# Split weight blocks of the projections: made once and kept in DRAM instead of made three times

## The chip, the cores and the metric

The kernel runs on one core of a Trainium2 chip. The metric is the device time of one execution in microseconds (us). The core has five engines with an instruction stream each: TensorE (PE, and PEld for its weight loads), VectorE (DVE), ScalarE (ACT), GpSimd (POOL) and SyncE (SP), which in this kernel issues nearly all DMA transfers. Each stream is worked off in order, and a semaphore wait of one instruction holds all that stand behind it.

## The reference

One layer of a decoder works on 2048 prompt tokens and on 8 sample sequences of 8 tokens, which share the weights. What is computed, in short:

```python
h    = rmsnorm(x, norm_mix_w)
proj = h @ w_in                                    # 1024 x 4096
rq, rk, rv, rg, hq, hf, hi, hg = split(proj, 8)    # 4 heads x 128 columns each
o_r  = retention(rotary(rq), rotary(rk), rv)       # decay 1 - 2^(-5-head), chunkwise
o_h  = hgrn2(silu(hq), 1 - f, hi, log(f))          # f = lb + (1 - lb) * sigmoid(hf)
o    = concat(head_rmsnorm(o_r) * silu(rg), head_rmsnorm(o_h) * silu(hg))
x    = x + o @ w_out                               # 1024 x 1024
x    = x + square(relu(rmsnorm(x, norm_ffn_w) @ w_up)) @ w_down
y    = rmsnorm(x, final_norm_w)
```

All of it is in float32. Results are y for both groups of tokens and the final states of both recurrences.

## The kernel before, in words

**Precision.** TensorE takes operands in a shorter format (fp32r). Each operand is therefore split into two parts: `hi`, the value rounded to fp32r, and `lo`, the rest. A product is three matmuls: hi x hi, hi x lo and lo x hi (`proj`, line 314).

**Groups.** The 2112 tokens are worked in three groups, each through the whole layer: group 0 (64 sample tokens and 512 prompt tokens), group 1 (768 prompt tokens) and group 2 (768). A group's activations stay on the chip. In each group come first the mix (for each of four heads p: `project` with four blocks of columns, `values` at line 672, and before the next head the two gate blocks, `gates`), then the output projection (`residual` at line 1110 with six weight blocks, and `out_proj_first` or `out_proj` with two), then the feed-forward part (`ffn_first` or `ffn`). `finish_first` and `finish`, the final norm of the group before, are spread over the first part of the next group's mix (DVE lines 1232 and 1605, stores of y at lines 1235 and 1607).

**The weight stream.** The weights lie in DRAM as blocks of 128 x 1024 float32, 512 KB each, in the order in which they are used; blocks 0 to 31 are the input projection's and 32 to 39 the output projection's (W_UP0 is 40). Every group uses these 40. `plan_stream` (line 273) lists all uses: 104 entries for group 0, then 149 for each of the others, in all 402. The feed-forward entries of groups 1 and 2 differ from those of group 0: they are for a product scheme with sums of blocks, which `plan_sums` forms during group 0 on VectorE (line 1256), stores in DRAM (line 1261) and which come back as entries of kind "s".

**What one entry costs.** `weight(i)` (line 242) is called when block i is about to be used, and it readies the blocks up to i + 2. For each: a DMA loads the block into a tile `raw` (line 251); ScalarE casts it to `hi` (line 256); VectorE or GpSimd subtracts, `lo = raw - hi` (line 271, `second_part`). GpSimd takes the subtraction where the entry says so, or, for the entries of these 40 blocks, where the stream number j is over 3 and not divisible by 4; VectorE takes the rest. `hi` and `lo` have three buffers each, so the cast of block i waits until TensorE has read block i - 3 for the last time. `raw` tiles have two buffers in group 0, and two and four more (tag `sum`) afterwards, where loads run further ahead.

**What uses two blocks at once.** `values` takes two blocks and holds both until its last matmul (line 687). All other uses take the blocks one after the other.

**Order.** Work beside the matmuls is put on an agenda counted in ticks (`at`, `later`, `tick`), a tick being a few matmuls. The framework then lays out each engine's instruction order with a time model of its own, from the order of the calls and from what is ready, with tiles taking their buffers in the order of the calls; `keep_in_program_order` pins single instructions behind what was called before on the same engine. All loads and stores that the prediction speaks of stand in the queue of SyncE.

**Lines that the prediction follows.** L610, L611 and L668: the halves of a projected key swapped on ScalarE, and times sine on GpSimd; L667 and L669: the rest of the rotation on VectorE. L823, L330, L331, L469 and L470: the product of query and key of the same token (GpSimd), its split (ScalarE, VectorE) and its column sums (TensorE). L777: the scan of the log gates on VectorE. L1292: the output projection's sums taken out of PSUM. L1588: sums of squares of the final norm on GpSimd.

Of the kernel before, what the change touches and what calls it, by code (L numbers as in the profile page):

```python
# [9 lines left out]
F32 = mybir.dt.float32  # L10
F32R = mybir.dt.float32r
# [4 lines left out]
P = 128  # L16
# [22 lines left out]
WT = 1024  # L39
N_IN, N_OUT, N_UP, N_DN = 32, 8, 32, 32  # L40
W_OUT0 = N_IN
W_UP0 = W_OUT0 + N_OUT
# [4 lines left out]
W_UQ0 = W_DN0 + N_DN  # L47
W_DQ0 = W_UQ0 + N_UP
NW = W_DQ0 + N_DN

# [91 lines left out]
def lay_out_weights(w_in, w_out, w_up, w_down):  # L144
    w = np.empty((NW, P, WT), np.float32)
    wi = w_in.reshape(KB, P, 8, H, DK)
# [51 lines left out]
class Kernel:  # L198
# [43 lines left out]
    def weight(self, i):  # L242
        n = len(self.stream)
        while self.w_next < min(i + 1 + self.ahead, n):
            j = self.w_next
            while self.w_load <= j or j >= self.n_first and self.w_load <= j + 2 and self.w_load < n:
                k, later = self.w_load, self.w_load >= self.n_first
                raw = self.raws[k] = self.wp.tile([P, WT], F32, tag="sum" if later and k % 3 else "raw", name="raw",
                                                  bufs=4 if later and k % 3 else 2)
                e = self.stream[k]  # L250
                self.fetch(raw, self.sums[e[1]] if e[0] == "s" else self.I["w"][e[1]])
                self.w_load += 1
            raw = self.raws.pop(j)
            hi = self.wp.tile([P, WT], F32R, tag="hi", name="hi")
            lo = self.wp.tile([P, WT], F32R, tag="lo", name="lo")
            self.nc.scalar.copy(hi, raw)  # L256
            self.wts[j] = (hi, lo)
            self.second[j] = raw
            pool = self.stream[j][2] if len(self.stream[j]) > 2 else j % 4 and 3 < j
            if pool or j < 4:  # L260
                self.second_part(j, self.nc.gpsimd if pool else self.nc.vector)
            else:
                self.later(4, self.second_part, j, self.nc.vector)
            self.w_next += 1
        self.second_part(i, self.nc.vector)
        return self.wts[i]
# [6 lines left out]
    def plan_stream(self):  # L273

        self.stream = [("w", j) for j in range(W_UP0)]
        up = [[("w", W_UP0 + 4 * t + i) for i in range(4)] for t in range(NQ)]
        dn = [[("w", W_DN0 + 4 * t + i) for i in range(4)] for t in range(NQ)]
        self.stream += up[0]
        for t in range(NQ):
            self.stream += (up[t + 1] if t < NQ - 1 else []) + dn[t]  # L280
        self.n_first = len(self.stream)

        def entry(name, key, i0, pool):
            return ("s", key + (name,), pool) if name[0] == "S" else ("w", i0 + A_PLACE[name], pool)

        for g in range(1, len(GROUPS)):
            self.stream += [("w", j) for j in range(W_UP0)]
            self.stream += [("w", W_UQ0 + i, i % 2) for i in range(4)]
            for t in range(1, NQ):
                self.stream += [entry(name, ("u", t), W_UQ0 + 4 * t, name in ("A12", "S1", "S4")) for name, _ in PRODUCTS]  # L290
            for o in range(NO):
                for k, (name, *_) in enumerate(LAST_OCTET if o == NO - 1 else OCTET):
                    end = g == len(GROUPS) - 1 and o == NO - 1 and k > 4
                    self.stream += [entry(name, ("d", o, v), W_DQ0 + 4 * (2 * o + v), not end and (2 * k + v) % 5 in (1, 3))
                                    for v in range(2)]

    def next_weight(self):
        i = self.w_use
        self.w_use += 1
        r = self.weight(i)  # L300
        self.wts.pop(i - 4, None)
        return r

# [45 lines left out]
    def build(self):  # L349
        nc, tc, I = self.nc, self.tc, self.I  # L350
        with ExitStack() as ctx:
# [10 lines left out]
            self.raws, self.sums, self.side = {}, {}, deque()  # L362
            self.ordered = True
            self.ahead = 2
            self.wts, self.second = {}, {}
            self.blocks = deque()
            self.plan_stream()

# [1365 lines left out]
```

## Time and profile before

| | |
|---|---|
| median of 3 runs | 2627.51 us |
| lowest and highest | 2626.79 and 2630.17 us |
| the profiled execution | 2629.84 us |
| its span, first to last instruction | 2628.0 us |
| mean granted TensorE clock | 0.995 |
| TensorE busy | 2570.6 us |
| VectorE, ScalarE, GpSimd busy | 1683.9, 1234.5, 1089.9 us |
| moved by DMA | 365.81 MB, mean 139 GB/s |

In this execution the groups lie as follows, by the first and last instructions of their lines: group 0's mix until about 300 us, its output projection until 368, its feed-forward part until 793; group 1's mix until about 1150, its output projection until 1222, its feed-forward part until 1697; group 2 from there.

A row of groups reads: line, engine, operation, output <- inputs, shapes, count; busy us in all, mean ns of one; idle us before them and what ended it. A row of the timeline reads: start, length, engine (a q behind it: its sequencer, such as SPq when a DMA is issued), line, operation, tiles, shapes, how many in a row, and in brackets the idle time before and what ended it. A row of the stretches gives the busy time of TensorE, its weight loads, VectorE, ScalarE and GpSimd (instructions in brackets), then the clock, the mean busy share of the 16 DMA engines and their GB/s. A matmul's time there is that from issue to end; neighbours overlap.

### The profile page before, as it was taken

How to read it: one execution, taken by the hardware profiler on the slowest of the kernel's cores; microseconds unless marked ns; L12 is line 12 of the kernel's file. 1: busy time of each engine (PE TensorE's matmuls, PEld its weight loads, DVE VectorE, ACT ScalarE, POOL GpSimd, SP SyncE). 2: the span in 40 equal slices, each digit the busy share in tenths (PEclk: the TensorE clock that was granted, in tenths of full speed). 3: DMA queues.
4: the chain of work that ended last, by engine and by line, in shares of the span. 5: the costliest groups of instructions: out<-in, count | busy, mean ns of one | idle time of the engine just before them, and what ended most of it. 6: DMA issues, size and time to landing. Idle time of an engine off the chain costs nothing. (4 is left out here: it accounts for less than half of the span.)

```text
span 2628.0 us, 41634 instructions
## 1 busy us (share of the span) xinstructions
PE 2570.6 (98%) x16999; PEld 2536.8 (97%) x16999; DVE 1683.9 (64%) x2077; ACT 1234.5 (47%) x1653; POOL 1089.9 (41%) x605
## 2 busy tenths in 40 slices
PE   8999999999999999999999999999999999999997
PEld 8999999999999999999999999989999999999997
DVE  6666776545565466565554988675665665549886
ACT  6555442222244555554543545455555445345443
POOL 6555557444436355431222332463554302223322
PEclk9999999999999999999999999999999999999999
DMA  5233366666752111122556755421111225566552
GB/s 181 81 97 90 121 217 241 232 252 221 266 183 85 57 49 49 53 66 69 166 174 203 261 169 199 145 97 49 46 44 59 70 69 178 179 207 209 175 178 81
DMA packets 125951, 365.81 MB, mean 139 GB/s; under 512 B 12480, under 2 KB 33984, under 8 KB 125760
## 3 DMA queue, kind: packets, MB, share of 16 engines
q1 hardware_dynamic: 125616, 363.13, 41.7%
q8 instruction: 134, 2.20, 0.3%
q14 instruction: 57, 0.47, 0.1%
q10 hardware_dynamic: 144, 0.02, 0.0%
HBM read 293.10 MB, written 69.99 MB: 138 GB/s over the span
## 5 line engine op out<-in xcount | busy, mean ns | idle before, releaser
L271 POOL TENSOR_TENSOR lo<-raw,hi 128x1024 fp32r<-128x1024 f32 x227 | 591.3, 2605 | 1257.6 <-ACT hi L256 1140.6
L323 PE MATMUL pj<-slab,hi 128*128 128x288 f32 (+1 forms) x5120 | 1016.8, 316 | 18.9 <-ACT hi L256 6.3
L323 PEld LDWEIGHTS pj<-slab,hi 128*128 128x128 f32 x5120 | 811.8, 189 | 25.2 <-ACT hi L256 9.3
L256 ACT CAST hi<-raw 128x1024 fp32r<-128x1024 f32 x402 | 422.3, 1052 | 847.1 <-PE pj L323 373.3
L323 PE MATMUL pj<-slab,lo 128*128 128x288 f32 (+1 forms) x2560 | 600.1, 315 | 1.8 <-POOL lo L271 1.7
L1105 PE MATMUL pd<-slab,hi 128*128 128x384 f32 x1792 | 457.2, 335 | 6.7 <-DVE slab L1551 3.1
L323 PEld LDWEIGHTS pj<-slab,lo 128*128 128x128 f32 x2560 | 430.0, 189 | 2.9 <-POOL lo L271 2.0
L1105 PE MATMUL pu<-slab,hi 128*128 128x384 f32 x1600 | 396.2, 334 | 0.0
L1105 PEld LDWEIGHTS pd<-slab,hi 128*128 128x128 f32 x1792 | 324.3, 188 | 8.4 <-DVE slab L1551 3.7
L271 DVE TENSOR_TENSOR lo<-raw,hi 128x1024 fp32r<-128x1024 f32 x175 | 231.6, 1323 | 156.0 <-ACT hi L256 152.7
L1105 PE MATMUL pd<-slab,lo 128*128 128x384 f32 x896 | 300.2, 335 | 0.9 <-POOL lo L271 0.9
L1105 PEld LDWEIGHTS pu<-slab,hi 128*128 128x128 f32 x1600 | 288.2, 188 | 0.0
L1105 PE MATMUL pu<-slab,lo 128*128 128x384 f32 x800 | 256.9, 334 | 0.0
L687 PE MATMUL pjv<-hi,slab 128*128 128x256 f32 x1088 | 211.6, 288 | 3.9 <-DVE slab L667 3.9
L1307 DVE TENSOR_TENSOR slab<-slab 128x768 fp32r<-128x768 f32 x144 | 162.3, 1143 | 41.4 <-ACT slab L1303 29.1
L687 PEld LDWEIGHTS pjv<-hi,slab 128*128 128x128 f32 x1088 | 175.5, 193 | 5.6 <-DVE slab L667 4.3
L1105 PEld LDWEIGHTS pd<-slab,lo 128*128 128x128 f32 x896 | 168.8, 188 | 1.5 <-POOL lo L271 1.5
L1303 ACT CAST slab<-slab 128x768 fp32r<-128x768 f32 x144 | 117.9, 833 | 108.3 <-DVE slab L1314 84.9
L687 PE MATMUL pjv<-lo,slab 128*128 128x256 f32 x544 | 155.0, 285 | 0.0
L1105 PEld LDWEIGHTS pu<-slab,lo 128*128 128x128 f32 x800 | 149.3, 188 | 0.0
L1521 DVE TENSOR_TENSOR slab<-pd,slab 128x768 f32<-128x768 f32 x110 | 104.1, 950 | 40.0 <-PE pd L1105 39.7
L797 ACT ACTIVATE slab<-slab 128x768 f32<-128x768 f32 (+2 forms) x72 | 56.3, 781 | 135.8 <-POOL slab L793 135.7
(197 smaller groups left out, 3405.2 us busy)
## 6 DMA issues: line engine op xcount, KB each, us to landing
raw<-w SPq DMA_DIRECT2D x342, 512.0 KB, 3.9
u<-ld SPq DMA_DIRECT2D x64, 384.0 KB, 4.6
slab<-u SPq DMA_DIRECT2D x64, 384.0 KB, 5.8
ld<-x SPq DMA_DIRECT2D x32, 384.0 KB, 4.6
y<-slab SPq DMA_DIRECT2D x12, 384.0 KB, 2.5
raw<-su1S SPq DMA_DIRECT2D x8, 512.0 KB, 3.7
raw<-su2S SPq DMA_DIRECT2D x8, 512.0 KB, 3.9
raw<-su3S SPq DMA_DIRECT2D x8, 512.0 KB, 4.0
```

The lines of the kernel that those rows point to most:

```text
L256: self.nc.scalar.copy(hi, raw)
L271: eng.tensor_tensor(out=lo, in0=self.second.pop(j), in1=hi.bitcast(F32), op=ALU.subtract)
L323: self.nc.tensor.matmul(pj[:, i, :T2], w, a[:, c0:c1], start=j == 0 and q == 0, stop=j == n - 1 and q == 2)
L687: nc.tensor.matmul(pj[:, i * 256:(i + 1) * 256], a[:, s:s + C], ww, start=kb == 0 and q == 0, stop=kb == KB - 1 and q == 2)
L797: nc.scalar.activation(x["dd", w][:, a:T], x["dd", w][:, a:T], AF.Exp)
L1105: self.nc.tensor.matmul(*a, **k)
L1303: self.nc.scalar.copy(hi[:, :g.T], B[name][:, :g.T])
L1307: self.nc.vector.tensor_tensor(out=lo[:, :g.T], in0=B[name][:, :g.T], in1=hi.bitcast(F32)[:, :g.T], op=ALU.subtract)
L1521: nc.vector.tensor_tensor(out=r, in0=ps, in1=r, op=ALU.add)
```

## The change

Blocks 4 to 39 (from N_MADE = 4 on) are split only by group 0. When group 0 takes such a block, it also issues two DMA stores, which write `hi` and `lo` to tiles in DRAM that live until the end (`self.kept`). In groups 1 and 2 the stream's entries for them are of kind "p": `weight` gives them `hi` and `lo` tiles and loads both from DRAM, with no `raw` tile, no cast and no subtraction. Blocks 0 to 3, and all feed-forward blocks, are treated as before. When the loader looks ahead for raw tiles, it stops at an entry of kind "p". The new transfers are issued by SyncE and are not pinned. So 72 casts, 72 subtractions and 72 loads of 512 KB go; 72 stores and 144 loads of 512 KB come.

```diff
+N_MADE = 4
...
         while self.w_next < min(i + 1 + self.ahead, n):
             j = self.w_next
+            e = self.stream[j]
+            if e[0] == "p":
+
+                self.wts[j] = tuple(self.wp.tile([P, WT], F32R, tag=tag, name=tag) for tag in ("hi", "lo"))
+                for part, kept in zip(self.wts[j], self.kept[e[1]]):
+                    self.nc.sync.dma_start(part.bitcast(F32), kept)
+                self.w_next += 1
+                self.w_load = max(self.w_load, j + 1)
+                continue
             while self.w_load <= j or j >= self.n_first and self.w_load <= j + 2 and self.w_load < n:
+                if self.stream[self.w_load][0] == "p":
+                    break
                 k, later = self.w_load, self.w_load >= self.n_first
...
         for g in range(1, len(GROUPS)):
-            self.stream += [("w", j) for j in range(W_UP0)]
+            self.stream += [("p" if j >= N_MADE else "w", j) for j in range(W_UP0)]
...
         i = self.w_use
         self.w_use += 1
         r = self.weight(i)
+        if N_MADE <= i < W_UP0:
+            self.kept[i] = [self.dp.tile([P, WT], F32, name=f"w{i}{part}") for part in ("hi", "lo")]
+            for part, kept in zip(r, self.kept[i]):
+                self.nc.sync.dma_start(kept, part.bitcast(F32))
         self.wts.pop(i - 4, None)
         return r
...
-            self.wts, self.second = {}, {}
+            self.wts, self.second, self.kept = {}, {}, {}
```

## The prediction

> **What bounds the kernel now.** I read the page first, then the busy time by stretch, then TensorE's own waits, then the order in time around those waits, and the DMA queue last.
>
> ```profile
> span 2628.0 us, 41634 instructions
> PE 2570.6 (98%) x16999; PEld 2536.8 (97%) x16999; DVE 1683.9 (64%) x2077; ACT 1234.5 (47%) x1653; POOL 1089.9 (41%) x605
> L271 POOL TENSOR_TENSOR lo<-raw,hi 128x1024 fp32r<-128x1024 f32 x227 | 591.3, 2605 | 1257.6 <-ACT hi L256 1140.6
> L256 ACT CAST hi<-raw 128x1024 fp32r<-128x1024 f32 x402 | 422.3, 1052 | 847.1 <-PE pj L323 373.3
> L271 DVE TENSOR_TENSOR lo<-raw,hi 128x1024 fp32r<-128x1024 f32 x175 | 231.6, 1323 | 156.0 <-ACT hi L256 152.7
> ```
>
> TensorE is busy for 2570.6 of 2628.0 us, and the change touches none of its matmuls. The weight splits are idle most of the time, the casts waiting for TensorE to release a buffer: they run ahead of need. So the ceiling of the gain is TensorE's idle time where splits disappear. That is the mix and the output projection of groups 1 and 2, and I cut the span into stretches to see it (us, then busy per engine, clock, DMA share, GB/s):
>
> ```profile
> 14.00:300.00 286.00, 281.65 (x2203) 270.93 (x2202) 192.65 (x330) 166.95 (x270) 171.50 (x142) 1.00 0.32 97
> 300.00:368.00 68.00, 65.24 (x482) 62.50 (x482) 49.09 (x75) 25.93 (x43) 20.50 (x11) 1.00 0.67 223
> 810.00:1200.00 390.00, 384.03 (x2646) 377.83 (x2645) 229.69 (x367) 201.42 (x288) 187.34 (x111) 1.00 0.19 59
> 1760.00:2118.00 358.00, 355.78 (x2445) 350.25 (x2444) 215.09 (x342) 185.40 (x263) 157.87 (x95) 1.00 0.19 57
> ```
>
> Rows three and four are where groups 1 and 2 mix: 98 and 99% busy. Row one is group 0's mix, row two its output projection. What TensorE waits for from 793 to 1222, then from 1700 to 2140 (total, times, longest):
>
> ```profile
> PE mm L470 <- DVE slab L331: 3.9, 4, 1.8
> PE pj L323 <- DVE slab L1292: 2.3, 2, 1.2
> PE pjv L687 <- DVE slab L667: 1.5, 1, 1.5
> ...
> PE mm L470 <- DVE slab L331: 4.2, 4, 2.1
> PE pjv L687 <- DVE slab L667: 2.4, 1, 2.4
> PE pj L323 <- DVE slab L1292: 2.3, 2, 1.2
> ```
>
> No row names a weight (L256, L271). All wait for VectorE, 16.6 us in all. So whatever the change gives comes indirectly, through what runs on the other engines beside these chains.
>
> **The change part by part.** *Removed in groups 1 and 2:* for 36 blocks each, 72 casts, 72 subtractions and 72 raw loads. By the page's means that is 72 x 1.052 = 75.7 us of ScalarE; 54 subtractions on GpSimd, 54 x 2.605 = 140.7 us; 18 on VectorE (stream numbers divisible by 4), 18 x 1.323 = 23.8 us. Directly on the path: nothing. Indirectly, there are two kinds of gap.
>
> The first is at L470, once per head. Around the one at 929.33 us:
>
> ```profile
> 918.13 1.05 ACT L256 CAST hi<-raw 128x1024 fp32r<-128x1024 f32 x1 [2.74 <-PE pj L323]
> 919.26 2.40 POOL L271 TENSOR_TENSOR lo<-raw,hi 128x1024 fp32r<-128x1024 f32 x1 [4.86 <-ACT hi L256]
> 921.62 1.85 POOL L668 TENSOR_TENSOR slab<-slab,ld 128x768 f32<-128x768 f32 x1
> 923.42 1.96 POOL L823 TENSOR_TENSOR slab<-slab 128x768 f32<-128x768 f32 x1
> 921.71 5.21 DVE L777 TENSOR_TENSOR_SCAN slab<-reset,slab 128x128 f32<-128x128 f32 x6
> 927.69 1.58 DVE L331 TENSOR_TENSOR slab<-slab 128x768 fp32r<-128x768 f32 x1
> 929.33 0.45 PE L470 MATMUL mm<-slab,ones_r 128*128 128x384 f32 x1 [0.69 <-DVE slab L331]
> L777 DVE TENSOR_TENSOR_SCAN slab<-reset,slab x64: 392/394/2611, 43.2 to 2019.0; 128x128 f32<-128x128 f32 x64
> ```
>
> On GpSimd L668 starts the moment L271 ends, and L823 right after it. The six scans beside them take 5.21 us, although one takes 0.39 us at its median: they are held while GpSimd works. Without the cast and the subtraction L668 starts up to 1.05 us and more earlier, GpSimd is through at least 1 us earlier, so are the scans and L331 behind them; the gap is 0.69 us. Of the eight L470 gaps (3.9 + 4.2 us) the two longest (1.8 and 2.1) stand at the groups' starts; the other six are 4.2 us together. I take these six as gone: -4.2. Bounds: 0 if the new program's order puts L470 forward by as much, -4.2 otherwise.
>
> The second is at the start of a group, where VectorE is full:
>
> ```profile
> 1735.01 11.24 DVE L1605 SCALAR_TENSOR_TENSOR slab<-slab,vec 128x384 f32<-128x384 f32 x11
> 1737.01 2.47 POOL L271 TENSOR_TENSOR lo<-raw,hi 128x1024 fp32r<-128x1024 f32 x1 [3.85 <-ACT hi L256]
> 1736.00:1747.00 11.00, 8.82 (x74) 8.61 (x72) 11.00 (x11) 4.21 (x5) 6.71 (x3) 1.00 0.42 155
> L1605 DVE SCALAR_TENSOR_TENSOR slab<-slab,vec x24: 602/613/2759, 1735.0 to 2610.5; 128x384 f32<-128x384 f32 x24
> 1747.17 0.58 PE L687 MATMUL pjv<-hi,slab 128*128 128x256 f32 x1 [2.35 <-DVE slab L667]
> 1752.55 0.45 PE L470 MATMUL mm<-slab,ones_r 128*128 128x384 f32 x1 [2.12 <-DVE slab L331]
> 1753.87:1757.28 3.41, 3.41 (x18) 3.41 (x17) 3.41 (x5) 1.49 (x4) 3.41 (x4) 0.50 0.00 0
> ```
>
> Eleven L1605 take 11.24 us where 0.61 each would make 6.7, and L667 stands behind them. One 2.47 us subtraction leaves GpSimd inside that burst. In that stretch GpSimd works 6.71 us (the last time in the row from 1736 to 1747; VectorE's there is 11.00), and VectorE takes 11.24 - 6.7 = 4.5 us too long: two thirds of GpSimd's time is VectorE's loss. 0.67 x 2.47 = 1.6, which I round to 1.5 us. Group 1's start has the same burst with L1232, and its L687 gap is 1.5 us. So -1.5 twice, -3.0; bounds 0 and the 7.8 us of all four start gaps. The second gap follows from VectorE's own chain behind L667 and stays. The last row shows the clock at half for 3.41 us after those gaps; I count nothing for it, and if one such stretch goes, 1.7 us go with it.
>
> The Trainium skill, page "SBUF — State Buffer", section "Who interferes with whom", says that a VectorE instruction with two SBUF inputs is fully blocked by a GpSimd instruction that reads SBUF, not slowed. By it the whole 2.47 us would come back in each burst, -1.5 and -2.35 instead of -3.0, and the sum below would be lower by 0.9; the 2.6 us that one scan took at most agree with it.
>
> The L1292 waits in the output projection (2.3 + 2.3 us) stay: what VectorE does there is not removed.
>
> *Added in groups 1 and 2:* 144 loads of 512 KB, two for each block. Each waits on SyncE for TensorE's last read of the block three before.
>
> ```profile
> raw<-w SPq DMA_DIRECT2D x342, 512.0 KB, 3.9
> 941.13 1.05 ACT L256 CAST hi<-raw 128x1024 fp32r<-128x1024 f32 x1
> 951.87 1.05 ACT L256 CAST hi<-raw 128x1024 fp32r<-128x1024 f32 x1 [1.43 <-PE pj L323]
> 350.00:370.00 20.00, 17.24 (x126) 16.56 (x125) 18.09 (x21) 8.51 (x11) 2.79 (x2) 1.00 0.94 328
> SPq L1607 <- DVE slab L1605: 58.7, 12, 30.4
> ```
>
> The tightest place is behind a value projection, which releases two blocks at once: the second of two casts shows both buffers free by 941.13 at the latest, and the next release, at 951.87, is when TensorE turns to the first of the new blocks. That leaves 10.7 us. One load lands 3.9 us after its issue; the rate of 328 GB/s at a share of 0.94, so 349 GB/s when full, makes 1.5 us of all engines for 512 KB, so the pair has landed some 5.8 us after release. Hidden, with 5 us to spare; elsewhere there are two blocks' time. The loader now also stops at these blocks when it looks ahead, so the first raw loads of the feed-forward part are asked for two blocks before their use and not earlier: with 3.9 us to land, hidden too. The share there, 0.19, has room for 36 x 1.5 = 54 us more in 390. Cost 0; bounds 0 and, with that cover gone, up to a few us at each of eight value projections.
>
> *Added in group 0:* 72 stores. A store waits for both halves of a block, which TensorE needs by then anyway, and what is queued behind it on SyncE is the next raw load, which waits for the same subtraction already. In the mix 56 stores are 84 us against 0.68 x 286 = 194 free. In the output projection 16 are 24 us, against 0.33 x 68 = 22.4 free: 1.6 us too many. I take +1.6; bounds 0 and, if loads behind stores are late one for one, 16.
>
> **Sum:** -4.2 - 3.0 + 1.6 = -5.6 us. The profiled execution took 2629.84 us, 1.84 beside its span, and is 2.33 above the median of the three runs, 2627.51. So 2624.2 in its own time, and **2621.9 us** as the median.
>
> **The rivals.** *No gain.* The order of the instructions on every engine is worked out anew for the changed program; where a chain gets shorter, the matmul that needs it may be put forward by as much, and the same gap stands again. For it: all gaps are short and of one kind, as if the order were tight on a guess that is too short by a fixed part. Against it: the cause, GpSimd beside VectorE, is partly gone. Time: 2627.5 + 1.6 = 2629.1.
>
> *SyncE in order.* The loads stand in one queue with the stores of y, which wait for L1605 (58.7 us in 12 waits). At group 2's start:
>
> ```profile
> 1751.01 10.12 SPq L1607 DMA_DIRECT2D y<-slab  x3
> 1763.57 2.02 ACT L256 CAST hi<-raw 128x1024 fp32r<-128x1024 f32 x2
> ```
>
> The last of three stores ends its issue at 1761.1. The loads of the first gate block, placed behind it, would have landed 5.8 us later, at 1766.9; TensorE needs them when it leaves the value blocks, which the two casts show at 1763.6. 3.3 us lost, and perhaps a half-clock stretch, 1.7, more. Against it: TensorE releases that buffer before the stores are due. Time: 2621.9 + 5.0 = 2626.9.
>
> *Slower: the stores choke group 0's output projection.* From 350 to 370 us the DMA engines have a share of 0.94 already, with the first sums loaded and stored and the first feed-forward weights on their way. If the 24 us of stores push these back, the sums that VectorE forms in fixed order wait for their operands, and what empties PSUM waits behind them. The cover is 5 to 8 us: the load issued at 343.13 lands 3.9 us later by the page's median, 5.1 us ahead of its cast. It decides once more than this is pushed back. Price 24 - 8 = 16: 2627.5 - 7.2 + 16 = 2636.3.
>
> ```profile
> 343.13 0.33 SPq L231 DMA_DIRECT2D raw<-w  x1
> 352.11 1.05 ACT L256 CAST hi<-raw 128x1024 fp32r<-128x1024 f32 x1 [5.40 <-PE pj L323]
> ```
>
> Against it: the cast at 352.11 waits for TensorE (5.40 us), not for data. The Trainium skill, page "DMA: Bandwidth & Descriptors", section "Where 436 GB/s comes from", puts the limit of HBM for one core at about 358 GB/s; by it 8.4 MB of stores beside 223 GB/s fit into 68 us (346 GB/s), with no excess, and the sum would be -7.2.
>
> *More gain.* All start gaps close and the half-clock stretch goes with them, and the stores cost nothing: -4.2 - 7.8 - 1.7 = -13.7, 2613.8. For it: each instruction taken off GpSimd frees VectorE elsewhere too. Against it: three gaps of four would need VectorE's own work to shrink.
>
> **How the numbers follow.** Chances: forecast 0.40, more gain 0.14, no gain 0.14, SyncE 0.09, choked 0.23. A measurement of this kernel tells 0.2%, 5.3 us, from no change. The forecast stands at that edge (below 2622.2): I put 0.25 of its 0.40 on the fast side. Faster 0.25 + 0.14 = 0.39; same 0.15 + 0.14 + 0.08 = 0.37; slower 0.23 + 0.01 = 0.24. The range reaches from the larger gain, 2613, to the choked case, 2636.
>
> **What would show it.** Right: L470 <- L331 falls from eight waits to the two at the starts, L687 <- L667 under 1 us each, no TensorE wait names a DMA or hi, lo; GpSimd's busy time falls by about 140 us, ScalarE's by 75. Wrong: new waits of TensorE at L323 or L687 for DMA in groups 1 and 2 (loads late), gaps between 350 and 440 us (stores), or the same L470 gaps at new times (no gain).

## The result, and the profile after

| | before | after |
|---|---|---|
| median, runs taken side by side | 2627.15 us | 2614.46 us |
| lowest and highest of 4 runs | 2626.64 and 2630.17 | 2612.39 and 2617.13 |
| the profiled execution | 2629.84 | 2617.13 |
| its span | 2628.0 | 2615.4 |

The ratio is 0.995, with a 95% interval of 0.9933 to 0.9967: 12.7 us faster. The forecast was 2621.9 with a range of 2613 to 2636. The sign was right, and the gain is more than twice the forecast sum of 5.6 us; the time lies near the fast edge of the range, which was set by the case "more gain". Two more comparisons below gave 0.9947 and 0.9942.

Line numbers of the changed kernel: L269 is the cast (before: L256), L284 the subtraction (L271), L253 the new loads, L317 the new stores; from line 314 of before on, a number is higher by 17 (L331 is L348, L470 is L487, L667 and L668 are L684 and L685, L687 is L704, L777 is L794, L823 is L840, L1232 is L1249, L1605 is L1622).

The page after, in the columns of the page before:

```profile
span 2615.4 us, 41690 instructions
PE 2566.6 (98%) x16999; PEld 2535.8 (97%) x16999; DVE 1643.1 (63%) x2059; ACT 1161.6 (44%) x1581; POOL 953.1 (36%) x551
L284 POOL TENSOR_TENSOR lo<-raw,hi 128x1024 fp32r<-128x1024 f32 x173 | 459.4, 2656 | 1085.2 <-ACT hi L269 999.6
L269 ACT CAST hi<-raw 128x1024 fp32r<-128x1024 f32 x330 | 347.0, 1052 | 758.6 <-PE pj L340 323.7
```

GpSimd lost 54 instructions and 136.8 us, ScalarE 72 and 72.9 us. VectorE lost 18 instructions and 40.8 us, where 18 subtractions make 23.8: another 17 us went because what it still does ran faster. That is the first sign of where the time comes from. What TensorE waits for, group 1's mix and output projection first (785 to 1215 us), then group 2's (1690 to 2130):

```profile
PE pj L340 <- DVE slab L1309: 2.2, 2, 1.1
...
PE mm L947 <- DVE AT L854: 2.5, 1, 2.5
PE pj L340 <- DVE slab L1309: 2.2, 2, 1.1
PE mm L487 <- DVE slab L348: 2.2, 1, 2.2
```

Of the rows of before, the waits of L687 (now L704) for L667 (L684) are gone from both groups, and of eight waits of L470 (L487) one is left. No row names a DMA, L269, L284 or L253. One wait has grown: that of L947 for L854 in group 2 takes 2.5 us (before, as L930 for L837, 0.5 us in group 1 and 0.2 in group 2).

**Where the 12.7 us lie.** I cut each trace by the starts of TensorE's own landmarks: the first matmul of a head's values (L687), the last one, and the first transpose of a group's mix (L543). The table has the lengths in us; "first head's values" runs from their first matmul to their last, "other heads" from there to the last one of the fourth head's values.

| stretch | before | after | |
|---|---|---|---|
| start to the first values | 36.5 | 39.1 | +2.6 |
| group 0: its four heads' values | 241.9 | 241.9 | 0 |
| group 0: on to group 1's transposes | 504.3 | 503.7 | -0.6 |
| group 1: first head's values | 24.5 | 19.9 | -4.6 |
| group 1: other heads | 267.3 | 264.4 | -2.9 |
| group 2: first head's values | 28.2 | 25.1 | -3.1 |
| group 2: other heads | 267.3 | 264.4 | -2.9 |
| all the rest | 1258.0 | 1256.9 | -1.1 |

The first row is no part of the change: in that one run TensorE's clock came up later (at 14.1 us, in before at 9.7; the same program took 37.8 and 37.5 us in two other profiles). The gain stands in four stretches, two kinds of two: group starts, 7.7 us, and heads, 5.8 us. Smaller parts lie in the last row: 0.7 us between group 2's first transpose and its first values (46.9 to 46.2), and 0.4 us in each group from the last head's values to the feed-forward part (104.7 to 104.3).

**Group starts.** VectorE's burst and GpSimd beside it at group 1's start, before:

```profile
823.63 11.26 DVE L1232 SCALAR_TENSOR_TENSOR slab<-slab,vec 128x576 f32<-128x576 f32 x8
...
826.49 2.43 POOL L271 TENSOR_TENSOR lo<-raw,hi 128x1024 fp32r<-128x1024 f32 x1 [4.62 <-ACT hi L256]
828.87 2.37 POOL L668 TENSOR_TENSOR slab<-slab,ld 128x768 f32<-128x768 f32 x1
831.20 2.36 POOL L823 TENSOR_TENSOR slab<-slab 128x768 f32<-128x768 f32 x1
```

and after:

```profile
824.17 5.93 DVE L1249 SCALAR_TENSOR_TENSOR slab<-slab,vec 128x576 f32<-128x576 f32 x8
...
829.43 2.38 POOL L685 TENSOR_TENSOR slab<-slab,ld 128x768 f32<-128x768 f32 x1 [7.02 <-ACT slab L628]
831.77 1.96 POOL L840 TENSOR_TENSOR slab<-slab 128x768 f32<-128x768 f32 x1
```

The same eight operations take 5.93 us instead of 11.26. Counted from the start of the burst, GpSimd's L685 starts no earlier than L668 did (5.26 and 5.24 us). But before, the subtraction had held the burst up, so that L668 and L823 fell into it too: 7.2 us of GpSimd beside it, 5.3 us lost, 0.74 of it. After, the burst ends 0.7 us after L685 has begun. One removed instruction of 2.43 us takes nearly all the overlap with two more away.

In group 2's first values TensorE's idle gaps are no smaller: 2.35 + 2.12 + 0.19 before, 2.22 + 2.47 after, 4.7 both times. Yet the stretch is 3.1 us shorter. VectorE's burst and TensorE's stop at L487 (L470), after:

```profile
1728.16 5.38 DVE L1622 SCALAR_TENSOR_TENSOR slab<-slab,vec 128x384 f32<-128x384 f32 x10
...
1742.23 0.44 PE L487 MATMUL mm<-slab,ones_r 128*128 128x384 f32 x1 [2.22 <-DVE slab L348]
```

Ten operations take 5.38 us, where before eleven took 11.24. The chain behind them lets TensorE go on at L487 12.6 us after the first matmul of the values (at 1729.62); before it was 16.5 us (1752.55 from 1736.03). So VectorE's chain is 3.9 us shorter, and 0.8 us of it is lost again behind L487, where the wait of L947 has grown.

Two half-clock stretches of 3.41 us, at 1747.04 and 1753.87 us in before, are gone as well (TensorE at half its clock, 0.50). It would be tempting to put the 3.1 us down to them. The run e1_stores, which splits all blocks as before, speaks against it: its trace has only the second of them, and the stretch is 28.2 us all the same. TensorE reaches the stop sooner and waits longer there, 3.50 us instead of 2.12, and goes on 16.5 us after its first values (1735.30), as in before:

```profile
1751.83 0.44 PE L487 MATMUL mm<-slab,ones_r 128*128 128x384 f32 x1 [3.50 <-DVE slab L348]
```

**Heads.** The second head of group 1, the one shown in the prediction, after:

```profile
917.69 1.85 POOL L685 TENSOR_TENSOR slab<-slab,ld 128x768 f32<-128x768 f32 x1 [7.34 <-ACT slab L628]
919.50 1.96 POOL L840 TENSOR_TENSOR slab<-slab 128x768 f32<-128x768 f32 x1
...
918.46 4.55 DVE L794 TENSOR_TENSOR_SCAN slab<-reset,slab 128x128 f32<-128x128 f32 x6
923.78 1.58 DVE L348 TENSOR_TENSOR slab<-slab 128x768 fp32r<-128x768 f32 x1
...
925.76 0.34 PE L486 MATMUL mm<-slab,ones_r 128*128 128x384 f32 x1
925.94 0.34 PE L487 MATMUL mm<-slab,ones_r 128*128 128x384 f32 x1
```

GpSimd is idle for 7.34 us ahead of L685 instead of subtracting, the scans take 4.55 us instead of 5.21, and L487 follows L486 at once. Counted from the first matmul of this head's values (918.23 before, 915.70 after), VectorE's L331 (L348) starts at 9.5 us before and at 8.1 after. How much one such stop cost is seen in before, where the same pair of lines stands twice in a row, with the stop (the L470 between the first two rows is quoted in the prediction) and without:

```profile
928.30 0.33 PE L469 MATMUL mm<-slab,ones_r 128*128 128x384 f32 x1
...
929.61 0.28 PE L687 MATMUL pjv<-hi,slab 128*128 128x256 f32 x1
...
930.32 0.34 PE L469 MATMUL mm<-slab,ones_r 128*128 128x384 f32 x1
930.49 0.34 PE L470 MATMUL mm<-slab,ones_r 128*128 128x384 f32 x1
930.67 0.28 PE L687 MATMUL pjv<-hi,slab 128*128 128x256 f32 x1
```

From L469 to the matmul behind L470 it is 1.31 us with the stop and 0.35 without: the stop costs 0.96 us, although its idle time reads 0.69. Matmuls in a row overlap: those of 0.34 us start 0.17 us apart here. At a stop the last one runs out and the next one starts alone. Six times 0.96 is 5.8 us, what the two rows of heads lost.

**Stores and loads.** The stretch of group 0's output projection that I thought tightest, after:

```profile
350.00:370.00 20.00, 17.24 (x126) 16.55 (x125) 18.15 (x19) 6.33 (x8) 4.13 (x2) 1.00 1.00 366
```

The DMA engines are full (1.00, 366 GB/s; before 0.94 and 328), and TensorE is busy for the same 17.24 us with the same 126 matmuls.

### The profile page after: what moved, and what is told of

Read it like the earlier page. It is cut to its first block, busy times and chain, and to the rows that moved or that the text cites. A ratio compares the mean times of both kernels' runs of the same rounds, so it can differ in the third digit from the quotient of the medians.

```text
span 2615.4 us, 41690 instructions
## 1 busy us (share of the span) xinstructions
PE 2566.6 (98%) x16999; PEld 2535.8 (97%) x16999; DVE 1643.1 (63%) x2059; ACT 1161.6 (44%) x1581; POOL 953.1 (36%) x551
## 4 chain that ended last, share of the span: by engine, by line
PE 81%; DVE 4%; POOL 2%; issue 2%; ACT 1%; DMA 0%; DVEq 0%; SPq 0%; POOLq 0%; ACTq 0%
PE pj L340 36%; PE pu L1122 16%; PE pd L1122 14%; PE pjv L704 5%; PE mm L1122 2%; PE mm L833 1%; PE po L1014 1%; PE mm L1022 1%; PE po L1016 1%; POOL lo L284 1%; PE mm L890 1%; PE mm L487 1%; PE mm L486 1%; PE mm L765 0%; DVE slab L1538 0%
## 5 line engine op out<-in xcount | busy, mean ns | idle before, releaser
L340 PE MATMUL pj<-slab,hi 128*128 128x288 f32 (+1 forms) x5120 | 1018.5, 317 | 18.6 <-ACT hi L269 6.9
L284 POOL TENSOR_TENSOR lo<-raw,hi 128x1024 fp32r<-128x1024 f32 x173 | 459.4, 2656 | 1085.2 <-ACT hi L269 999.6
L340 PEld LDWEIGHTS pj<-slab,hi 128*128 128x128 f32 x5120 | 812.9, 190 | 25.4 <-ACT hi L269 6.1
L269 ACT CAST hi<-raw 128x1024 fp32r<-128x1024 f32 x330 | 347.0, 1052 | 758.6 <-PE pj L340 323.7
L340 PE MATMUL pj<-slab,lo 128*128 128x288 f32 (+1 forms) x2560 | 600.9, 316 | 2.0 <-POOL lo L284 1.8
L340 PEld LDWEIGHTS pj<-slab,lo 128*128 128x128 f32 x2560 | 430.4, 189 | 3.1 <-POOL lo L284 2.0
L284 DVE TENSOR_TENSOR lo<-raw,hi 128x1024 fp32r<-128x1024 f32 x157 | 207.0, 1319 | 145.7 <-ACT hi L269 142.3
L704 PE MATMUL pjv<-hi,slab 128*128 128x256 f32 x1088 | 208.5, 285 | 0.0
L704 PEld LDWEIGHTS pjv<-hi,slab 128*128 128x128 f32 x1088 | 173.4, 191 | 1.4
L704 PE MATMUL pjv<-lo,slab 128*128 128x256 f32 x544 | 153.8, 283 | 0.0
L1538 DVE TENSOR_TENSOR slab<-pd,slab 128x768 f32<-128x768 f32 x110 | 104.2, 950 | 37.6 <-PE pd L1122 37.4
L704 PEld LDWEIGHTS pjv<-lo,slab 128*128 128x128 f32 x544 | 103.8, 191 | 0.0
```

Of the source, the lines that this page charges most:

```text
L284: eng.tensor_tensor(out=lo, in0=self.second.pop(j), in1=hi.bitcast(F32), op=ALU.subtract)
L340: self.nc.tensor.matmul(pj[:, i, :T2], w, a[:, c0:c1], start=j == 0 and q == 0, stop=j == n - 1 and q == 2)
L704: nc.tensor.matmul(pj[:, i * 256:(i + 1) * 256], a[:, s:s + C], ww, start=kb == 0 and q == 0, stop=kb == KB - 1 and q == 2)
L1538: nc.vector.tensor_tensor(out=r, in0=ps, in1=r, op=ALU.add)
```

## Experiments

**Theory A:** the gain comes from GpSimd. Its subtractions held up VectorE, whose chains TensorE waits for at the groups' starts and in the heads. **Rivals:** that it is ScalarE's time, or the time in GpSimd's own order, or the fewer raw loads; that the stores take part of it back; that only one of the two places matters.

Each kernel ran in five rounds beside the kernel before. Medians in us:

| kernel | this | before | ratio, 95% interval |
|---|---|---|---|
| e0_after: the change | 2616.15 | 2630.39 | 0.9947, 0.9935 to 0.9960 |
| e1_stores: only the stores | 2630.32 | 2630.39 | 1.0002, 0.9994 to 1.0011 |
| e2_lo_kept: only lo kept | 2617.97 | 2630.39 | 0.9955, 0.9942 to 0.9969 |
| e3_hi_kept: only hi kept | 2651.74 | 2630.39 | 1.0082, 1.0069 to 1.0096 |
| e4_gp_add: subtractions given back to GpSimd | 2625.23 | 2629.67 | 0.9984, 0.9975 to 0.9993 |
| e5_gp_memset: GpSimd fills instead | 2614.59 | 2629.67 | 0.9944, 0.9932 to 0.9957 |
| e7_first6: blocks 4 to 9 only | 2623.43 | 2629.67 | 0.9976, 0.9966 to 0.9986 |
| e8_from10: blocks 10 to 39 only | 2622.96 | 2629.67 | 0.9976, 0.9967 to 0.9986 |
| e9_memset2: GpSimd fills twice | 2618.39 | 2630.99 | 0.9953, 0.9939 to 0.9967 |
| e6_made0: all forty blocks | 2626.02 | 2630.99 | 0.9976, 0.9966 to 0.9986 |
| e10_after: the change | 2615.40 | 2630.99 | 0.9942, 0.9929 to 0.9955 |

Their traces, cut as above (span at the end):

| | start | g0 heads | g0 rest | g1 first | g1 others | g2 first | g2 others | rest | span |
|---|---|---|---|---|---|---|---|---|---|
| before | 36.5 | 241.9 | 504.3 | 24.5 | 267.3 | 28.2 | 267.3 | 1258.0 | 2628.0 |
| e0_after | 37.8 | 241.9 | 502.6 | 19.9 | 264.4 | 25.1 | 264.4 | 1258.2 | 2614.4 |
| e10_after | 37.5 | 241.9 | 502.4 | 19.9 | 264.4 | 25.1 | 264.4 | 1257.2 | 2612.8 |
| e1_stores | 38.0 | 241.9 | 502.4 | 24.5 | 267.3 | 28.2 | 267.3 | 1259.7 | 2629.3 |
| e2_lo_kept | 37.4 | 241.9 | 502.4 | 20.7 | 265.2 | 25.9 | 266.3 | 1255.5 | 2615.3 |
| e3_hi_kept | 37.7 | 241.9 | 502.7 | 25.1 | 271.3 | 29.3 | 273.0 | 1269.0 | 2650.0 |
| e4_gp_add | 37.5 | 241.9 | 502.9 | 23.8 | 266.7 | 26.2 | 265.2 | 1259.0 | 2623.2 |
| e5_gp_memset | 37.5 | 241.9 | 505.4 | 20.0 | 264.4 | 23.9 | 264.4 | 1256.9 | 2614.4 |
| e9_memset2 | 37.5 | 241.9 | 505.4 | 20.4 | 264.5 | 25.2 | 264.5 | 1257.2 | 2616.6 |
| e7_first6 | 36.7 | 241.9 | 502.1 | 19.9 | 267.3 | 25.1 | 267.3 | 1256.8 | 2617.1 |
| e8_from10 | 37.8 | 241.9 | 505.5 | 24.4 | 264.4 | 28.2 | 264.4 | 1257.1 | 2623.7 |
| e6_made0 | 43.9 | 244.1 | 505.4 | 19.9 | 264.4 | 25.1 | 264.4 | 1257.0 | 2624.2 |

The heads repeat to 0.1 us between kernels that do the same there. The start, group 0's rest (with its feed-forward part) and the last column but one scatter by 1 to 3 us from trace to trace. In group 0's rest most of that goes with the half-clock stretches: one in the traces with 502.4 us, three in those with 505.4.

All diffs are against the changed kernel. Those of e2 and e3 show the main lines: these two kernels have no entries of kind "p" and store only the part that they keep. Line numbers differ from kernel to kernel; those of before are given beside them.

**e0_after and e10_after: the change again, as marks.** No edit.

> The changed kernel once more, as the mark for the others beside it: 0.995 of the kernel before, about 2614 us. If its executions fall into two sets some 4 us apart, the start of the clock (up at 9.7 or at 14.1 us) tells them apart, and not the change.

> The changed kernel itself, on the same chip and beside the same runs of the kernel before, as the mark for the two others: 2613 to 2617 by every theory.

2616.15 and 2615.40, 14.2 and 15.6 us under before; the first comparison gave 12.7. In the four stretches the three traces of the change agree to 0.1 us. Whether the start of the clock (12.3 and 11.6 us here) parts the executions, two traces do not show.

**e1_stores: the stores alone.** Group 0 writes the parts, and nobody loads them.

```diff
-            self.stream += [("p" if j >= N_MADE else "w", j) for j in range(W_UP0)]
+            self.stream += [("w", j) for j in range(W_UP0)]
```

> Group 0 stores both halves of blocks 4 to 39, and nobody loads them: groups 1 and 2 split their blocks as before. What the stores cost alone. My term of +1.6 us expects 2629 us (1.0006). The trace of the changed kernel (group 0's mix 241.9 us long in both, 503.7 against 504.3 us from its end to group 1's first transposes) expects nothing, within 1 us. The choked case would be 1.006.

The time and every stretch are those of before; group 0's columns are those of the change. The 72 stores cost nothing that can be measured. My +1.6 and the rival that they choke the output projection fall.

**e2_lo_kept: lo kept, hi made.** Groups 1 and 2 load raw and cast it as before, and load `lo`: the subtraction goes, ScalarE's cast and the raw load stay.

```diff
-            self.stream += [("p" if j >= N_MADE else "w", j) for j in range(W_UP0)]
+            self.stream += [("w", j) for j in range(W_UP0)]
...
             self.nc.scalar.copy(hi, raw)
+            if j >= self.n_first and e[0] == "w" and N_MADE <= e[1] < W_UP0:
+                self.nc.sync.dma_start(lo.bitcast(F32), self.kept[e[1]])
+                self.w_next += 1
+                continue
```

> Only lo is kept and loaded; the raw block is still loaded and cast by ScalarE in groups 1 and 2, so that the casts stay and the subtractions (54 on GpSimd, 18 on VectorE) go. Theory A, GpSimd's subtractions hold VectorE: nearly the whole gain, 0.995 to 0.996, -10 to -13 us. Theory B, ScalarE's casts hold the copies that feed GpSimd and VectorE: little of it, 0.999, -0 to -3 us.

0.9955 beside 0.9947: nearly the whole gain, with ScalarE as busy as before (1234.1 us). The stretches stand 0.8 to 1.9 us above those of the change, 4.3 in all, while the medians differ by 1.8. So the casts and the raw loads are worth a few us at most, and the subtractions the rest. Where the casts count is shown under e4.

**e3_hi_kept: hi kept, lo made.** The other half: no cast, but raw is loaded and the subtraction stays.

```diff
-            self.nc.scalar.copy(hi, raw)
+            if j >= self.n_first and e[0] == "w" and N_MADE <= e[1] < W_UP0:
+                self.nc.sync.dma_start(hi.bitcast(F32), self.kept[e[1]])
+            else:
+                self.nc.scalar.copy(hi, raw)
```

> Only hi is kept and loaded; the raw block is loaded too, and lo is subtracted as before, so that the subtractions stay and the 72 casts go. Theory A: 0.999 to 1.001, at most -3 us, since GpSimd works as long as before. Theory B: 0.995 to 0.997, -8 to -13 us. A third outcome, both halves of the change giving about half each, would speak for two causes that add up.

21 us slower than before, with 72 casts fewer: none of the three outcomes set down beforehand. The heads take 271.3 and 273.0 us, 9.7 more than in before; about as much again lies outside the heads and starts, most of it between group 2's last head and its feed-forward part (111.5 us, before 104.7). VectorE has the same 2077 instructions as before and is busy for 1752.2 us instead of 1683.9. From the end of group 2's last head in this trace: the longest wait of TensorE there, GpSimd, then VectorE (L340 is L331 of before, L277 the subtraction):

```profile
PE mm L757 <- DVE AT L869: 4.8, 1, 4.8
```

```profile
2049.32 2.70 POOL L944 TENSOR_TENSOR slab<-slab,con 128x768 f32<-128x768 f32 x1 [3.25 <-PE mm L939]
2051.98 3.09 POOL L277 TENSOR_TENSOR lo<-raw,hi 128x1024 fp32r<-128x1024 f32 x1
...
2050.24 8.81 DVE L340 TENSOR_TENSOR slab<-slab 128x768 fp32r<-128x768 f32 x4
2058.98 0.57 DVE L869 COPY_PREDICATED AT<-msk,mm 128x192 f32<-128x192 uint8 x1
```

Four L340 take 8.81 us beside GpSimd, 2.2 us each. In before the four at this place take 1.8 us each:

```profile
2035.56 7.06 DVE L331 TENSOR_TENSOR slab<-slab 128x768 fp32r<-128x768 f32 x4
```

L869 stands behind them, and TensorE behind that. The subtraction now waits for a DMA instead of a cast, and with it all that GpSimd has behind it; the longest of these waits is in group 1:

```profile
POOL lo L277 <- DMA hi<-w37hi: 23.0, 1, 23.0
```

So GpSimd's work falls at other times and, in the rows shown, beside other operations of VectorE, which is 68 us longer busy with the same instructions. That fits the theory: the same GpSimd work at other times costs 21 us. It does not prove it, since the waits for the DMA are new as well; which of the displaced operations cost how much was not taken apart.

**e4_gp_add: GpSimd's subtractions given back.** All of the change, and at the place where the subtraction was, GpSimd subtracts two constant tiles into the `lo` tile before it is loaded. 54 operations of 2.44 us, of the old shape.

```diff
                 self.wts[j] = tuple(self.wp.tile([P, WT], F32R, tag=tag, name=tag) for tag in ("hi", "lo"))
+                if j % 4:
+                    self.nc.gpsimd.tensor_tensor(out=self.wts[j][1], in0=self.con[:, :WT], in1=self.con[:, 512:512 + WT],
+                                                 op=ALU.subtract)
```

> The changed kernel with work put back on GpSimd: ahead of the loads of the 54 blocks that GpSimd used to subtract, it subtracts two tables of constants into the lo tile, which the load then overwrites. No cast, no subtraction on VectorE. GpSimd's instructions stand where they stood before. Theory A, GpSimd's time is what counts: the gain goes, 0.999 to 1.001. If the 18 subtractions taken off VectorE, or the casts, carried part of it, that part stays: 0.997.

2625.23: 10.6 us above e5, which ran beside it on the same chip. At group 1's start, GpSimd first:

```profile
825.35 2.47 POOL L253 TENSOR_TENSOR lo<-con 128x1024 fp32r<-128x1024 f32 x1 [4.60 <-PE pj L343]
827.79 2.36 POOL L688 TENSOR_TENSOR slab<-slab,ld 128x768 f32<-128x768 f32 x1
830.10 2.36 POOL L843 TENSOR_TENSOR slab<-slab 128x768 f32<-128x768 f32 x1
...
822.50 11.30 DVE L1252 SCALAR_TENSOR_TENSOR slab<-slab,vec 128x576 f32<-128x576 f32 x8
```

The burst is back at 11.30 us, with L688 and L843 (L668 and L823 of before) in it. Of the four stretches 8.1 us of 13.5 are back, and the ratio, 0.9984, lies between the two that were expected. What stays is in part the casts'. The start of L331 in group 1's third head, counted from the first matmul of the head's values, shows it:

| | cast | GpSimd's subtraction | L331 starts at |
|---|---|---|---|
| before | yes | yes | 9.4 us |
| e2_lo_kept | yes | no | 8.7 |
| e4_gp_add | no | yes, of constants | 8.7 |
| e5_gp_memset | no | fill instead | 8.1 |
| after | no | no | 8.0 |

In before the cast stands on ScalarE ahead of the copies L610 and L611, for which VectorE's L667 waits; without it L667 starts 0.7 us sooner (1.8 us in after, 2.6 in before and e2). The other five heads of groups 1 and 2 have the same times to 0.1 us. So in the heads cast and subtraction hold VectorE by some 0.7 us each, and either one gone closes the stop of 0.69 us at L470: no such wait is left in the heads of e2 or of e4. At the groups' starts it is the subtraction: group 1's first values take 20.7 us without it and with the cast, 23.8 with it and without the cast. The share of VectorE's 18 subtractions was not taken apart.

**e5_gp_memset: GpSimd fills instead of subtracting.** The same place and count, but an operation that reads nothing.

```diff
+                if j % 4:
+                    self.nc.gpsimd.memset(self.wts[j][1].bitcast(mybir.dt.bfloat16), 0.0)
```

> As the run before, but GpSimd fills the lo tile with zeros (no operand read; the tile seen as 2048 elements of two bytes, estimated at 2 us from 0.75 us for a fill of 128x768) in place of subtracting. It fills GpSimd's queue in the same places. If what counts is VectorE being held by what GpSimd reads: the gain stays, 0.995 to 0.996. If what counts is GpSimd's own queue, L668 and L823 standing behind: the gain goes as with the subtraction, 0.998 to 1.000.

2614.59, all of the gain. GpSimd's fill lies inside the burst and lengthens it by nothing (5.93 without; L687 on GpSimd is L668 of before):

```profile
827.85 1.81 POOL L253 MEMSET lo<- 128x2048 bf16 x1 [5.25 <-PE pj L342]
829.61 2.38 POOL L687 TENSOR_TENSOR slab<-slab,ld 128x768 f32<-128x768 f32 x1
...
824.36 5.92 DVE L1251 SCALAR_TENSOR_TENSOR slab<-slab,vec 128x576 f32<-128x576 f32 x8
```

The Trainium skill, page "SBUF — State Buffer", section "Who interferes with whom", says that a VectorE instruction with two SBUF inputs contends with a GpSimd instruction that reads SBUF, and not with one that only writes it. The trace agrees: 1.81 us of filling cost the burst nothing, 2.47 us of subtracting brought the loss back, with the operations behind them at the same place: 5.25 and 5.29 us after the burst's start (829.61 from 824.36, 827.79 from 822.50).

**e9_memset2: filled twice.** The fill is shorter than the subtraction (1.80 against 2.44 us), so time in GpSimd's order was still a rival. Two fills are longer.

```diff
+                for _ in range(2 if j % 4 else 0):
+                    self.nc.gpsimd.memset(self.wts[j][1].bitcast(mybir.dt.bfloat16), 0.0)
```

> As the kernel whose GpSimd filled the lo tile with a constant (1.80 us a block) at the place of the subtraction, but it fills it twice: 3.6 us a block, longer than the 2.44 us of the subtraction of constants that cost 9 us. It leaves the output right, since the load follows. Theory A (VectorE is held by GpSimd's operations that read tiles, and GpSimd's queue has room): 2613 to 2618, the eight operations of VectorE's burst at group 1's start still at 6 us. The rival C (it is the time that the operation takes in GpSimd's order, which delays what VectorE waits for): as much as the subtraction or more, 2625 to 2632.

2618.39, 3.0 us above the change beside it and 0.4 above what theory A expected; C's 2625 is far. GpSimd is now busier than in before (1089.9 us), and the burst is still free (L842 on GpSimd is L823 of before):

```profile
PE 2567.8 (98%) x16999; PEld 2536.8 (97%) x16999; DVE 1633.3 (62%) x2059; ACT 1162.1 (44%) x1581; POOL 1139.5 (44%) x659
```

```profile
831.93 1.80 POOL L253 MEMSET lo<- 128x2048 bf16 x1
833.69 1.89 POOL L842 TENSOR_TENSOR slab<-slab 128x768 f32<-128x768 f32 x1
...
824.36 5.92 DVE L1251 SCALAR_TENSOR_TENSOR slab<-slab,vec 128x576 f32<-128x576 f32 x8
```

The first fill lies in the burst as in e5, at 827.85. The second begins when the burst is over and pushes L842 back by 1.7 us (833.69; 831.95 with one fill); its share of the loss is the 3 us at most. So GpSimd's order has room for 3.6 us a block, and at the groups' starts it is not its time but the kind of its operation that costs. In the heads the two are not parted as cleanly: there the fill of 1.80 us ends sooner than the subtraction of 2.44, and with two fills VectorE's instructions stand in another order. Whether reading alone decides, or also the type written, e4 and e5 do not tell apart.

**e7_first6 and e8_from10: the two places apart.** Blocks 4 to 9 (behind the groups' starts) or 10 to 39 (the other heads and the output projection) are kept, the others made.

```diff
-            self.stream += [("p" if j >= N_MADE else "w", j) for j in range(W_UP0)]
+            self.stream += [("p" if N_MADE <= j < 10 else "w", j) for j in range(W_UP0)]
...
-        if N_MADE <= i < W_UP0:
+        if N_MADE <= i < 10:
```

```diff
-N_MADE = 4
+N_MADE = 10
```

> Only blocks 4 to 9 are kept and loaded: the two value blocks and the gate blocks around a group's start, the rest as before. My sum put -3.0 us on the groups' starts. The traces put -8.4 there (4.7 in group 1's first value projection, 0.6 and 3.1 in group 2's): 0.997, about -8 us.

> Only blocks 10 to 39 are kept and loaded. My sum put -4.2 us on the six gaps at L470 of heads 1 to 3; the traces put -5.9 on the six heads and -0.7 on the output projections: 0.9975, about -6.5 us. If the parts add up, this run and the one with blocks 4 to 9 make -14 together; if they don't, the gain hangs on the order of the instructions and not on the work taken away.

6.2 and 6.7 us, 12.9 together, somewhat less than the 8 and 6.5 expected. The table shows why they add: e7 has the starts of the change (19.9, 25.1) and the heads of before (267.3), e8 the starts of before (24.4, 28.2) and the heads of the change (264.4). Six of 36 blocks bring half of the gain.

**e6_made0: all forty blocks.** Could the first four be kept as well?

```diff
-N_MADE = 4
+N_MADE = 0
```

> All forty blocks are written by group 0 and loaded by groups 1 and 2 (N_MADE = 0): blocks 0 to 3 too. Theory A (the gain is what GpSimd's and VectorE's subtractions did to VectorE at the groups' starts and in the heads): VectorE loses eight subtractions of 1.3 us that stand ahead of the bursts, under the output stage of the group before, where TensorE waits for nothing of VectorE's; half a us to one us more than the changed kernel at most, 2612 to 2616. The rival B (group 0's first blocks meet its crowded start): eight more stores of 0.5 MB in the first 40 us, where the DMA engines are 80 to 97 in a hundred busy, are 4 MB more, some 10 us of their time; if all of that delays the first products, 2620 to 2626.

2626.02, 10.6 us above the change beside it. The starts and heads gain nothing (19.9, 25.1, 264.4), so blocks 0 to 3 did no harm where they were made. (Of the eight subtractions that go, two were VectorE's and six GpSimd's, by the counts of instructions, 2059 to 2057 and 551 to 545; the expectation puts all eight on VectorE.) The first stretch is 6.4 us longer and group 0's heads 2.2. The time is rival B's; for the first stretch its reason is less the engines' load than SyncE's order. SyncE in this kernel, ScalarE's wait that follows, and TensorE's:

```profile
1.65 0.42 SPq L233 DMA_DIRECT2D slab<-x  x1
6.16 0.33 SPq L317 DMA_DIRECT2D w0hi<-hi  x1
6.54 0.43 SPq L233 DMA_DIRECT2D slab<-x  x1
...
9.61 2.45 SPq L233 DMA_DIRECT2D slab<-x  x5
```

```profile
ACT slab L524 <- DMA slab<-x: 7.4, 2, 4.0
```

```profile
15.77 1.70 PE L340 MATMUL pj<-slab,hi 128*128 128x288 f32 x4 [3.12 <-ACT slab L524]
```

and SyncE in e10_after:

```profile
1.64 3.28 SPq L233 DMA_DIRECT2D slab<-x  x7
```

The store of block 0's `hi` waits for its cast until 6.16 us. The six loads of x behind it are issued from 6.54 to 12.06 instead of by 4.92, and from 2.1 to 6.2 us SyncE issues nothing. TensorE's two waits for x, 1.00 and 3.12 us, are one part of the price. The other is the clock, which falls back to half during the second of them; e10_after has no such stretch there. e6_made0:

```profile
13.28:20.10 6.82, 4.33 (x16) 3.98 (x17) 3.80 (x5) 5.16 (x7) 0.00 (x0) 0.50 0.84 326
```

6.82 us at half the clock are up to 3.4 us lost. The 2.2 us of group 0's heads were not taken apart.

## Why the prediction held, and where it missed

**What bounds the kernel: right.** TensorE did not wait for weights, and what it waited for were VectorE's chains. At the groups' starts GpSimd holds them, as e2, e4 and e5 show by three ways; in the heads GpSimd's subtraction and ScalarE's cast do, some 0.7 us each.

**Term 1, the heads: right in cause, too small in size.** Forecast -4.2, measured -5.8 (2.9 in each of two groups; e8 shows it alone). The cause named there, cast and subtraction both, is what e2 and e4 bear out. All six gaps closed, as assumed. The price was read from the idle column, 0.69 us each, where the stop costs 0.96.

**Term 2, the starts: the step that failed.** "So -1.5 twice, -3.0"; measured 4.6 and 3.1, 7.7 in all (e7 shows it alone). The factor, two thirds of GpSimd's time, was good (0.74). The mistake was to multiply it with one instruction's 2.47 us. In group 1 the freed burst ends 0.7 us after GpSimd's next instruction has begun, so the loss that is left is not two thirds of the other 4.7 us but nearly nothing. L687's gaps, forecast as under 1 us, vanished. Of the L470 gaps, forecast to stay, group 1's vanished too (1.76 us). Group 2's stayed by its idle time (2.12, now 2.22), but it ends 3.9 us sooner, and the wait at L947 grew from 0.19 to 2.47 us. The half-clock stretches, counted at nothing, were two in before, not one; e1 shows that one of them could go with no time gained.

I took "fully blocked" from the Trainium skill, page "SBUF — State Buffer", section "Who interferes with whom". It says of this pair that they contend, and of contention that it is an exclusive lock; its words on full blocking are about VectorE's two-port modes. The measured loss is smaller than full blocking for GpSimd's whole time: 5.3 us of 7.2.

**Term 3, the loads: right.** No wait of TensorE in groups 1 and 2 names them.

**Term 4, the stores: wrong, +1.6 against 0.** e1 has 1.0002. The surplus of 1.6 us was worked out from a mean rate, and DMA engines that are full for 20 us (1.00, 366 GB/s) made nothing late that TensorE needed. The 366 GB/s are also above the 358 GB/s that the prediction quotes as the limit of HBM for one core; the measurement decides.

**The rivals.** No gain: refuted; the order was laid out anew, and the gaps did not come back in the heads. SyncE in order: not here, no wait names L253; but e6 shows that mechanism at the program's start, for 6.4 us. Stores that choke: refuted by e1. More gain, -13.7: this is the one that came by size, with -12.7, -14.2 and -15.6 in three comparisons, and what I held against it, that three gaps of four would need VectorE's own work to shrink, is what happened: the burst of group 1 shrank by 5.3 us. That its sum fits so well is in part luck. It had all four start gaps closing, of which one stayed and another came; it had 1.7 us for a half-clock stretch; and it had the heads at 4.2 us instead of 5.8.

## What to carry to other kernels

When two engines hold each other up, do not price a removed instruction by its own length: ask which later instructions overlapped only because of the delay, and look at which operations, not how many us, stand beside the critical chain. Price a stop of TensorE from start to start, with and without it, not by its idle column. And before stores are put into the queue that issues the loads, look at what is behind the first of them: thirty-six blocks' stores were free, the stores of the first four cost 8.6 us in the trace of e6.

## What the runs showed of the hardware

A fill on GpSimd left a VectorE burst at 5.92 us, a subtraction of 2.47 us in its place, with the two operations that it let in, took it to 11.30.

Half-clock stretches of 3.41 us followed some stops of 2 us and not others, and the traces show what decides. In all 13 of them every change of the clock, once it has come up (at 9.66 us in before, 14.07 in after), comes a whole number of steps of 3.41 us later. What counts is how long TensorE is idle within one such step. A step with 1.94 us or more of idle time was followed by a half-clock step every time, one with less than 1.74 us never; in between there are cases of both. In before the stops of 2.35 and 2.12 us fall into one step each, which then has 2.22 and 2.10 us of idle time (the length of the step less TensorE's busy time):

```profile
1743.63:1747.04 3.41, 1.19 (x10) 0.98 (x9) 3.41 (x6) 0.83 (x1) 0.09 (x1) 1.00 0.53 195
1750.45:1753.87 3.42, 1.32 (x9) 1.33 (x10) 3.33 (x4) 0.84 (x1) 3.42 (x4) 1.00 0.31 115
```

In the change the stops of 2.22 and 2.47 us each lie across the end of a step. The most idle time that one step has there is 1.86 us, and no half-clock stretch follows:

```profile
1751.46:1754.87 3.41, 1.55 (x13) 1.55 (x14) 3.41 (x7) 0.62 (x2) 0.90 (x1) 1.00 0.83 304
```

In e5 the stop of 2.23 us at the same place falls into one step and a stretch follows. So the moment at which the clock comes up has a part in it, and the same stop can cost a stretch in one execution and none in another. A lost stretch is not always lost time: in e1 and before the first values of group 2 take the same 28.2 us, because VectorE's chain sets the end.

The step has the length of the free-running window of some 3.4 us that the Trainium skill names, page "TensorE: Matmul & The Clock Gate", section "What's actually happening". The rule that the same page gives in "HAM oscillation — how this bites in real kernels", no idle gaps over some 3.4 us, was not enough here, where a stop of 2.12 us sufficed.
